# The low-rank decay product written as one 96-row fp32r product, and a different bank for the pooling mix

## The chip, the cores and the metric

The kernel runs on one core of one Trainium2 chip. The core has five engines with a queue each: TensorE (PE in the profile; PEld is its weight load), VectorE (DVE), ScalarE (ACT), GpSimd (POOL) and SyncE (SP), which issues all DMA transfers of this kernel. The metric is the device time of one execution in microseconds (us); the time before is 1222.71 us, the median of three runs (1220.06, 1222.71, 1222.97). PE writes into PSUM, which this kernel divides into banks of 128 partitions x 512 fp32 values; ACT and DVE read a bank and so free it.

## The reference, cut to what matters

One block of a streaming encoder for 1024 tokens and 16 meta tokens, model width 1024. The input is normalised and projected by one wide matrix into `a` (512 columns), `q`, `k` (256), `v`, `r` (512), `lr` (16) and two gates (1024). What the change touches is the decay of the gated linear attention, which comes from the 16 columns `lr`, and the mixing of the pooled `a`, 128 columns to a group:

```
z = einsum('bld,dn->bln', u, w_in)
a, q, k, v, r, lr, ga, gb = split(z, ...)
p = multiscale_pool(a).reshape(B, L, 4, 128)
p = einsum('blgc,gce->blge', p, w_pool_mix).reshape(B, L, 512) * pool_scale
log_a = log_sigmoid((lr @ w_gate_up + b_gate).astype(float32)) / GLA_TAU
...
h = h + hybrid_mixer(rmsnorm(h, norm_mix), ...)
h = h + squared_relu_mlp(rmsnorm(h, norm_ffn), w_ff1, w_ff2)
return rmsnorm(h, norm_final)[:, N_META:]
```

`w_gate_up` has 16 rows and 256 columns, so `lr @ w_gate_up` sums over 16 terms only.

## The kernel before, in words

Most products are made from split operands: a value x is written as hi + lo, where hi is x rounded to fp32r and lo is the rest, and a product is hi·hi + hi·lo + lo·hi, three fp32r matmuls that accumulate in one bank (`mm3`, L280 to L282). The exception here is `log_decay` (L514): it multiplies the unsplit fp32 tiles `wgu` (16 x 256) and `gB[:16]` (the transposed `lr`, 16 x 1024), and `lrT_meta` for the meta tokens, as plain fp32.

The first part of the program is a list of steps, `one`, that `drive` runs through. `start` normalises and transposes the input into `th`/`tl`, makes `v` and `lr` together (`v_tile`, whose last 16 columns go to `lrtok`), and ends with `lr_turn`: three transposes of `lrtok` into `ms` banks, which ACT copies to `lrT_meta` and `gB[:16]` (L415, L420). `pool_open` releases the buffers of `start` and makes those of the pooling stage. Then follow blocks of projections and the work between them: `a_block(0)`, `decays(0)`, `a_block(1)`, `decays(1)`, `mix_block(0)`, `a_block(2)`, `mix_block(1)`, `a_block(3)`, `mix_block(2)`, `k_block(0)`, `mix_block(3)`, the differences, `k_block(1)`, and then the pairs of the remaining projections.

- `a_block` and `k_block` call `project`: three pieces of 264, 264 and 512 columns, 24 products each, every piece in one of the three `mm` banks in turn. ACT evicts each piece (L563 or L597).
- `decays(p)` calls `log_decay` for two halves of 512 columns and for the 16 meta columns, each in one of the three `ms` banks. ACT adds the bias (L515) and makes the logarithm of a sigmoid from absolute value, exponential and logarithm (L516 to L518), DVE joins them (L519), ACT takes the exponential (L528) and SP writes the decays to memory (L529). SP reads them back much later into the tile `g` (L925).
- `mix_block(g)` makes trailing sums of `a` on DVE (L576, L579), splits them into `ph` (ACT L582, DVE L583) and multiplies them by `mw`, one half in an `ms` bank and one in half of the wide pair `sc` (L280 to L282 again, output `b_ms` and `b_sc`). ACT scales both by `pool_scale` (L588).

The order of PE is that of the program as written (PE alone is scheduled by hand). The order of the other engines' queues is made by the framework's scheduler when the kernel is built; each engine then works through its queue strictly in order. Tiles lie on two stacks, left and right; a new tile on a place that was released waits until all users of the old one are done. The weights of the next blocks are split two blocks ahead by ACT (L84) and DVE (L85).

Of the kernel before, what the change touches and what calls it, by code (L numbers as in the profile page):

```python
# [7 lines left out]
F32 = mybir.dt.float32  # L8
F32R = mybir.dt.float32r
U8 = mybir.dt.uint8  # L10
ACT = mybir.ActivationFunctionType
ALU = mybir.AluOpType
AX = mybir.AxisListType

P = 128
D = 1024
SEQ = 1024
META = 16
KT = D // P
HALF = 512  # L20
# [102 lines left out]
def kernel(  # L123
# [3 lines left out]
    nc = tc.nc  # L127
# [3 lines left out]
    w_gate_up, b_gate, gla_norm, w_gla_out, w_out = w_gate_up[0], b_gate[0], gla_norm[0], w_gla_out[0], w_out[0]  # L131
    norm_ffn, w_ff1, w_ff2 = norm_ffn[0], w_ff1[0], w_ff2[0]

    act, dve, pool, pe = nc.scalar, nc.vector, nc.gpsimd, nc.tensor
    left, right = Stack(tc, "left"), Stack(tc, "right")
# [18 lines left out]
    def bank(tag):  # L154
        if tag == "sc":
            sc_n[0] += 1
            return two("sc")[:, sc_n[0] % 2]
        return psp[tag].tile([P, 512], F32, name=f"b_{tag}", tag=tag)
# [25 lines left out]
    gB = left.push("gB", [P, D], F32)  # L184
# [10 lines left out]
    stat = [tiny(16) for _ in range(4)]  # L195
    eps_t = tiny(1)
    pool.memset(eps_t, EPS)
    wgu = left.push("wgu", [16, 256], F32)
    metab = left.push("metab", [P, 5, 16], F32)
    lrT_meta = left.push("lrT_meta", [16, META], F32)  # L200
    raw = Raw(nc, [left.push(f"raw{i}", [P, D], F32) for i in range(2)])
    W1 = Ring(tc, raw, left.push("w1h", [P, 2, D], F32R), left.push("w1l", [P, 2, D], F32R), 2)
    left_ff = left.mark()
# [8 lines left out]
    def f32(ap):  # L212
        return ap.bitcast(F32)

    def col(v, n):
        return v.rearrange("(h p) -> p h", p=P)
# [87 lines left out]
    S, rings = {}, [W1]  # L304
# [56 lines left out]
    def nxt(key):  # L361
        i = S["n" + key]
        S["n" + key] += 1
        return S[key][:, i % S["d" + key]]

    def halves():
        return [slice(h * HALF, (h + 1) * HALF) for h in range(2)]
# [42 lines left out]
            nc.sync.dma_start(v_dram[i, t], o)  # L410

    def lr_turn():
        b = bank("ms")
        pe.transpose(b[:16, :16], S["lrtok"][:16, 8], ident[:16, :16])
        act.activation(lrT_meta, b[:16, :16], ACT.Copy)  # L415
        for h in range(2):
            b = bank("ms")
            for t in range(4):
                pe.transpose(b[:16, t * P : (t + 1) * P], S["lrtok"][:, 4 * h + t], ident)
            act.activation(gB[:16, h * HALF : (h + 1) * HALF], b[:16], ACT.Copy)  # L420


    SPREAD = {
# [7 lines left out]
    def start():  # L431
        act.preload_act_table_set("natural_log_exp_and_others")
        xs = left.push("xs", [P, 4, D], F32)
        us = left.push("us", [P, 3, D], F32)
        S["lrtok"] = left.push("lrtok", [P, 10, 16], F32)
        S["lrraw"] = left.push("lrraw", [P, KT, 16], F32)
        xm = left.push("xm", [META, D], F32)
        um = left.push("um", [META, D], F32)
        mf = left.push("mf", [P, 6, CH], F32)
        S["xr"] = right.push("xr", [P, KT, SEQ], F32)  # L440
        S["vw"] = [right.push(f"vw{i}", [P, 2, KT, n], F32R) for i, n in enumerate((VP, 256))]
        buffer("vo", 3, 2 * P, right)
        load = lambda t: nc.sync.dma_start(xs[:, t % 4], x[t * P : (t + 1) * P, :])
        blank = S["xr"].rearrange("p k c -> p (k c)")[:, -640:]
        pool.memset(blank, 0.0)

        def warm(n, cols=HALF):
            for _ in range(n):
                pe.matmul(bank("ms")[:, :cols], blank[:, HALF:], blank[:, :cols], start=True, stop=True)

        load(0)
        nc.sync.dma_start(um[:1], norm_mix[None, :])
        nc.sync.dma_start(ident, ident_in)
        ask_vw(0)
        nc.sync.dma_start(S["lrraw"], w_in[:, C_LR : C_LR + 16].rearrange("(k p) c -> p k c", p=P))
        pool.memset(xm[:1, :P], 1.0)
        warm(2)
        for c in halves():
            b = bank("mm")
            pe.matmul(b, xm[:1, :P], um[:1, c], start=True, stop=True)  # L460
            dve.tensor_copy(gB[:, c], b)
        warm(2)
        for t in range(8):
            if 0 < t < 6:
                load(t + 2)
            if t == 1:
                nc.sync.dma_start(xm, meta)
            if t == 3:
                W1.top_up()
            u = us[:, t % 3]  # L470
            layer_norm(xs[:, t % 4], u)
            transposed(u, t // 4, OFF[t // 4] + (t % 4) * P, ("ms", "sc"))
            if t == 0:
                load(1)
                load(2)
                warm(10, P)
                load_vw(0)
                ask_vw(1)
            if t == 6:
                layer_norm(xm, um)  # L480
            if t == 1:
                warm(6, P)
            if t == 2:
                load_vw(1)
            if t < 3:
                v_tile(0, t)
            else:
                for i, n in SPREAD[t]:
                    v_tile(i, n)
        transposed(um, 0, 0)  # L490
        v_tile(0, 7)
        v_tile(1, 6)
        v_tile(1, 7)
        v_tile(0, 8)
        v_tile(1, 8)
        lr_turn()
        nc.sync.dma_start(mf, masks)
        pool.tensor_copy(mask, mf)
        nc.sync.dma_start(pscale, col(pool_scale, 4))
        nc.sync.dma_start(bgate, col(b_gate, 2))  # L500
        nc.sync.dma_start(gnorm, col(gla_norm, 4))
        nc.sync.dma_start(wgu, w_gate_up)

    one = []
    step(one, start)
# [5 lines left out]
    def log_decay(lrT, p, n, y, t):  # L511

        b = bank("ms")[:, :n]
        pe.matmul(b, wgu[:, p * P : (p + 1) * P], lrT, start=True, stop=True)  # L514
        act.activation(y, b, ACT.Identity, bias=bgate[:, p : p + 1])  # L515
        act.activation(t, y, ACT.Abs)  # L516
        act.activation(t, t, ACT.Exp, scale=-1.0)
        act.activation(t, t, ACT.Ln, bias=1.0)  # L518
        dve.scalar_tensor_tensor(y, y, 0.0, t, ALU.min, ALU.subtract)  # L519

    META_LOG = (0, 3)

    def decays(p):
        def fn():
            for half, c in enumerate(halves()):
                y = nxt("c")
                log_decay(gB[:16, c], p, HALF, y, nxt("t1"))
                act.activation(y, y, ACT.Exp, scale=1.0 / TAU)  # L528
                nc.sync.dma_start(decay_dram[p, half], y)  # L529
                yield 0.6  # L530
            if p:
                act.activation(gnorm, gnorm, ACT.Copy, scale=0.5)
            log_decay(lrT_meta, p, META, metab[:, META_LOG[p]], metab[:, 4])
            if p:
                tc.keep_in_program_order(act.preload_act_table_set("exp_and_others"))

        return fn

    def pool_open():
        left.pop_to(base)  # L540
        right.pop_to(1)
        buffer("c", 4)
        buffer("t1", 3)
        S["left_t"] = left.mark()
        buffer("a", 2, 1056)
        buffer("s", 2, 1056)
        S["ph"] = left.push("ph", [P, 2, SEQ], F32R)
        mw = S["mw"] = left.push("mw", [P, 2, 4, P], F32R)
        r = raw.load(w_pool_mix.rearrange("g c e -> c g e"), 4 * P).rearrange("p (g e) -> p g e", g=4)
        act.activation(mw[:, 0], r, ACT.Copy)  # L550
        dve.tensor_tensor(mw[:, 1], r, f32(mw[:, 0]), ALU.subtract)
# [17 lines left out]
    def mix_block(g):  # L569
        def fn():  # L570
            a, w, e = pooled[g], WINDOWS[g], SEQ + META
            cur, k = a, 1
            while k < w:
                c = META - (w - 2 * k)
                dst = nxt("s")
                dve.tensor_tensor(dst[:, c:e], cur[:, c:e], cur[:, c - k : e - k], ALU.add)  # L576
                cur, k = dst, 2 * k
            pp = nxt("s")
            dve.scalar_tensor_tensor(pp[:, :SEQ], cur[:, META:e], 1.0 / w, a[:, META:e], ALU.mult, ALU.subtract)  # L579
            wb = (S["mw"][:, 0, g], S["mw"][:, 1, g])  # L580
            for c in halves():
                act.activation(S["ph"][:, 0, c], pp[:, c], ACT.Copy)  # L582
                dve.tensor_tensor(S["ph"][:, 1, c], pp[:, c], f32(S["ph"][:, 0, c]), ALU.subtract)  # L583
            for h, (tag, c) in enumerate(zip(("ms", "sc"), halves())):
                b = bank(tag)
                mm3(b, 1, lambda i: wb, lambda i: (S["ph"][:, 0, c], S["ph"][:, 1, c]))
                o = nxt("c")
                act.activation(o, b, ACT.Copy, scale=pscale[:, g : g + 1])  # L588
                nc.sync.dma_start(pm_dram[g, h], o)
                yield  # L590

        return fn
# [1044 lines left out]
```

## Time and profile before

| | value |
|---|---|
| time, median of 3 runs | 1222.71 us |
| time of the profiled execution | 1222.77 us |
| span of its instructions | 1221.0 us |
| mean granted TensorE clock | 0.999 |
| ACT busy | 572.0 us (47%) |
| DVE busy | 838.9 us (69%) |
| POOL busy | 75.5 us (6%) |
| PE busy on L514, the decay products with `gB` | 4.0 us, 8 instructions |

The span runs from the first to the last instruction of the profiled execution; the 1.77 us around it belong to the time too. In rows of a time line the columns are the start, the duration, the engine, the line, the operation, output and inputs with shapes, the count, and in square brackets how long the engine sat idle before it and what released it. In the chain of waits a row has the start, the length that the piece adds to the chain, and the piece. Durations of matmuls overlap, since they are pipelined: what a matmul costs in a row of others is the distance of starts, which is what the chain shows.

### The profile page before, as it was taken

The numbers are of one execution on the slowest core, as the hardware profiler recorded it, in microseconds if no ns is written. First come the engines' busy times: TensorE is split into PE (matmuls) and PEld (weight loads), VectorE is DVE, ScalarE is ACT, GpSimd is POOL, SyncE is SP. The second block draws the span as 40 slices with busy tenths as digits, with TensorE's granted clock in tenths as the row PEclk, the third lists the DMA queues.
The fourth block names the chain that finished last, engine by engine and source line by source line (L and its number), as shares of the span: only waits on it lengthen the run. The fifth ranks groups of instructions, "written<-read, shape, count | busy, mean of one in ns | idle before, by whom it ended". The sixth has DMA issues, their size and how long they took to land.

```text
span 1221.0 us, 18366 instructions
## 1 busy us (share of the span) xinstructions
PE 1207.9 (99%) x6807; PEld 997.2 (82%) x6807; DVE 838.9 (69%) x1381; ACT 572.0 (47%) x1009; POOL 75.5 (6%) x96
## 2 busy tenths in 40 slices
PE   9999999999999999999999999999999999999997
PEld 6998977778778888788778888888888888888886
DVE  6535657665777569825887677676775887887686
ACT  7627444444456224314655455454554444444544
POOL 0000043222330000000000000000000000000000
PEclk9999999999999999999999999999999999999999
DMA  8313334435247977921244444444569973333532
GB/s 236 93 40 95 118 100 130 147 105 164 81 137 266 318 243 233 323 67 69 104 139 156 141 163 151 150 155 145 172 228 326 332 246 104 96 95 96 171 95 88
DMA packets 153356, 192.76 MB, mean 158 GB/s; under 512 B 12178, under 2 KB 88226, under 8 KB 153267
## 3 DMA queue, kind: packets, MB, share of 16 engines
q1 hardware_dynamic: 153266, 191.59, 48.9%
q8 instruction: 53, 0.87, 0.3%
q14 instruction: 37, 0.30, 0.1%
HBM read 128.62 MB, written 62.93 MB: 157 GB/s over the span
## 4 chain that ended last, share of the span: by engine, by line
PE 89%; DVE 4%; DMA 2%; ACT 2%; issue 2%; POOL 0%; SPq 0%; POOLq 0%; ACTq 0%; DVEq 0%
PE b_mm L280 7%; PE b_mm L282 7%; PE b_mm L281 7%; PE b_y L280 6%; PE b_y L282 6%; PE b_y L281 6%; PE b_oa L282 5%; PE b_oa L281 5%; PE b_oa L280 5%; PE b_z L280 4%; PE b_z L282 4%; PE b_z L281 4%; PE b_sc L280 4%; PE b_ob L281 4%; PE b_ob L282 4%; PE b_ob L280 4%
## 5 line engine op out<-in xcount | busy, mean ns | idle before, releaser
L685 ACT ACTIVATE w1h<-raw 128x512 fp32r<-128x512 f32 x106 | 65.9, 622 | 59.3 <-PE b_y L281 25.3
L686 DVE TENSOR_TENSOR w1l<-raw,w1h 128x512 fp32r<-128x512 f32 x106 | 72.4, 684 | 22.0 <-ACT w1h L685 22.0
L280 PE MATMUL b_sc<-th,w1h 128*128 128x512 f32 x216 | 85.6, 396 | 0.6 <-ACT u2p L1420 0.6
L280 PE MATMUL b_z<-th,w1h 128*128 128x512 f32 x216 | 85.3, 395 | 0.5 <-DVE c L804 0.3
L281 PE MATMUL b_sc<-tl,w1h 128*128 128x512 f32 x216 | 84.9, 393 | 0.0
L281 PE MATMUL b_z<-tl,w1h 128*128 128x512 f32 x216 | 84.3, 390 | 0.4 <-DVE tl L1306 0.4
L282 PE MATMUL b_sc<-th,w1l 128*128 128x512 f32 x216 | 84.4, 391 | 0.0
L685 ACT ACTIVATE w1h<-fs 128x512 fp32r<-128x512 f32 x81 | 51.1, 631 | 70.7 <-PE b_y L281 32.9
L282 PE MATMUL b_z<-th,w1l 128*128 128x512 f32 x216 | 84.1, 389 | 0.0
L686 DVE TENSOR_TENSOR w1l<-fs,w1h 128x512 fp32r<-128x512 f32 x81 | 57.1, 705 | 26.1 <-ACT w1h L685 25.9
L280 PE MATMUL b_mm<-th,w1h 128*128 128x512 f32 (+1 forms) x208 | 72.1, 347 | 0.0
L281 PE MATMUL b_mm<-tl,w1h 128*128 128x512 f32 (+1 forms) x208 | 71.0, 341 | 0.0
L282 PE MATMUL b_mm<-th,w1l 128*128 128x512 f32 (+1 forms) x208 | 71.0, 341 | 0.0
L685 ACT ACTIVATE w1h<-bt 128x512 fp32r<-128x512 f32 x46 | 29.1, 632 | 70.9 <-issue 43.9
L1496 DVE TENSOR_TENSOR bt<-w,w 128x512 f32<-128x512 f32 x80 | 54.6, 683 | 1.0 <-DMA w<-in_w_ff_dram 0.9
L280 PE MATMUL b_mm<-wo,th 128*128 128x512 f32 x128 | 50.4, 393 | 0.0
L282 PE MATMUL b_mm<-wo,tl 128*128 128x512 f32 x128 | 49.9, 390 | 0.0
L281 PE MATMUL b_mm<-wo,th 128*128 128x512 f32 x128 | 49.8, 389 | 0.0
L280 PE MATMUL b_y<-wo,w1h 128*128 128x512 f32 x128 | 49.8, 389 | 0.0
L281 PE MATMUL b_y<-wo,w1h 128*128 128x512 f32 x128 | 49.8, 389 | 0.0
L282 PE MATMUL b_y<-wo,w1l 128*128 128x512 f32 x128 | 49.8, 389 | 0.0
L686 DVE TENSOR_TENSOR w1l<-bt,w1h 128x512 fp32r<-128x512 f32 x46 | 31.7, 690 | 25.6 <-ACT w1h L685 25.6
(405 smaller groups left out, 3334.6 us busy)
## 6 DMA issues: line engine op xcount, KB each, us to landing
hf_dram<-h SPq DMA_DIRECT2D x112, 256.0 KB, 2.1
raw<-hf_dram SPq DMA_DIRECT2D x112, 256.0 KB, 2.6
w<-in_w_ff_dram SPq DMA_DIRECT2D x64, 256.0 KB, 4.5
raw<-in_w_in_dram SPq DMA_DIRECT2D x22, 512.0 KB, 4.3
raw<-in_w_ff_dram SPq DMA_DIRECT2D x16, 512.0 KB, 4.2
rawx<-in_w_ff_dram SPq DMA_DIRECT2D x16, 512.0 KB, 4.2
rawp<-in_w_in_dram SPq DMA_DIRECT2D x10, 512.0 KB, 4.4
xs<-in_x_dram SPq DMA_DIRECT2D x8, 512.0 KB, 4.8
```

What stands on the lines that cost most here:

```text
L280: pe.matmul(ps, ah, bh, start=first and i == 0, stop=False, skip_group_check=more)
L281: pe.matmul(ps, ah, bl, start=False, stop=False, skip_group_check=more)
L282: pe.matmul(ps, al, bh, start=False, stop=last and i == n - 1, skip_group_check=more)
L685: act.activation(hi, a, ACT.Copy)
L686: dve.tensor_tensor(lo, a, f32(hi), ALU.subtract)
L1496: dve.tensor_tensor(bt, w, S["w2"][q[3:]][:, i], ALU.add if q[2] == "+" else ALU.subtract)
```

## The change

The decay product is now made from split operands as well, but in one matmul and not three. A tile `lr` with 96 rows holds the rounded `lr` in rows 0 to 15 and again in rows 64 to 79, and its rest in rows 32 to 47; all other rows are zero. A tile `gu` with 96 rows holds `w_gate_up` rounded in rows 0 to 15 and 32 to 47, and its rest in rows 64 to 79. The sum over the 96 rows is hi·hi + lo·hi + hi·lo. Both tiles are fp32r. They lie on the right stack, where the weights of `v` lay, so the call of `lr_turn` moves from the end of `start` into `pool_open`, behind the release. `wgu` is loaded three times by DMA into a tile of 96 rows that POOL has zeroed, and `lr` is zeroed by POOL as well. `wgu` takes as much room per partition as before and `metab` grows by the room that `lrT_meta` had, so that the tiles behind them keep their places. Apart from this, the first half of each mixing product goes to an `mm` bank instead of an `ms` bank.

```diff
-    wgu = left.push("wgu", [16, 256], F32)
-    metab = left.push("metab", [P, 5, 16], F32)
-    lrT_meta = left.push("lrT_meta", [16, META], F32)
+    wgu = left.push("wgu", [96, 256], F32)
+    metab = left.push("metab", [P, 6, 16], F32)
...
     def lr_turn():
+        def stacked(to, b):
+            act.activation(to[:16], b, ACT.Copy)
+            act.activation(to[64:80], b, ACT.Copy)
+            dve.tensor_tensor(to[32:48], b, f32(to[:16]), ALU.subtract)
+
         b = bank("ms")
         pe.transpose(b[:16, :16], S["lrtok"][:16, 8], ident[:16, :16])
-        act.activation(lrT_meta, b[:16, :16], ACT.Copy)
-        for h in range(2):
+        stacked(S["lr"][:, SEQ : SEQ + META], b[:16, :16])
+        for h, c in enumerate(halves()):
             b = bank("ms")
             for t in range(4):
                 pe.transpose(b[:16, t * P : (t + 1) * P], S["lrtok"][:, 4 * h + t], ident)
-            act.activation(gB[:16, h * HALF : (h + 1) * HALF], b[:16], ACT.Copy)
+            stacked(S["lr"][:, c], b[:16])
...
         pool.memset(blank, 0.0)
+        pool.memset(wgu, 0.0)
...
-        lr_turn()
...
-        nc.sync.dma_start(wgu, w_gate_up)
+        for r in (0, 32, 64):
+            nc.sync.dma_start(wgu[r : r + 16], w_gate_up)
...
-        pe.matmul(b, wgu[:, p * P : (p + 1) * P], lrT, start=True, stop=True)
+        pe.matmul(b, S["gu"][:, p * P : (p + 1) * P], lrT, start=True, stop=True)
...
-                log_decay(gB[:16, c], p, HALF, y, nxt("t1"))
+                log_decay(S["lr"][:, c], p, HALF, y, nxt("t1"))
...
-            log_decay(lrT_meta, p, META, metab[:, META_LOG[p]], metab[:, 4])
+            log_decay(S["lr"][:, SEQ : SEQ + META], p, META, metab[:, META_LOG[p]], metab[:, 4])
...
     def pool_open():
+        right.pop_to(1)
+        S["lr"] = right.push("lr", [96, SEQ + 2 * META], F32R)
+        S["gu"] = right.push("gu", [96, 256], F32R)
+        pool.memset(f32(S["lr"]), 0.0)
+        lr_turn()
+        act.activation(S["gu"], wgu, ACT.Copy)
+        dve.tensor_tensor(S["gu"][64:96], wgu[64:], f32(S["gu"][64:96]), ALU.subtract)
         left.pop_to(base)
-        right.pop_to(1)
...
-            for h, (tag, c) in enumerate(zip(("ms", "sc"), halves())):
+            for h, (tag, c) in enumerate(zip(("mm", "sc"), halves())):
```

PE has as many instructions as before in the same order; only operands and banks differ. This is PE's queue where the second decay block meets the first mixing block, before and of the change (`b_mm`, `b_ms` and `b_sc` are banks, line numbers of the changed file are one lower in `mm3`):

```order
L282 MATMUL b_mm<-th_144,w1l 128x512
L514 MATMUL b_ms<-gB,wgu 128x512 x2
L514 MATMUL b_ms<-lrT_meta,wgu 128x16
L280 MATMUL b_ms<-ph,mw 128x512
L281 MATMUL b_ms<-ph,mw 128x512
L282 MATMUL b_ms<-ph,mw 128x512
L280 MATMUL b_sc<-ph,mw 128x512
```

```order
L281 MATMUL b_mm<-th_140,w1l 128x512
L519 MATMUL b_ms<-lr,gu 128x512 x2
L519 MATMUL b_ms<-lr,gu 128x16
L279 MATMUL b_mm<-ph,mw 128x512
L280 MATMUL b_mm<-ph,mw 128x512
L281 MATMUL b_mm<-ph,mw 128x512
L279 MATMUL b_sc<-ph,mw 128x512
```

No row has moved; the decay products read `lr` and `gu`, and the mixing product of the first half writes an `mm` bank.

On ACT the place is the end of `start` and the beginning of the first projection block: `mw` are the mixing weights, `t2h` is a split operand of a later stage, `a` the evictions of the first two pieces. Before, and of the change:

```order
L550 ACTIVATE mw<-raw_120 128x512
L406 ACTIVATE gB<-b_mm 16x256 x2
L415 ACTIVATE lrT_meta<-b_ms 16x16
L615 ACTIVATE t2h<-xr 128x2048
L420 ACTIVATE gB<-b_ms 16x512 x2
L563 ACTIVATE a<-b_mm 128x264 x2
```

```order
L561 ACTIVATE mw<-raw_116 128x512
L550 ACTIVATE gu<-wgu 96x256
L405 ACTIVATE gB<-b_mm 16x256 x2
L413 ACTIVATE lr<-b_ms 16x16
L414 ACTIVATE lr<-b_ms 16x16
L626 ACTIVATE t2h<-xr 128x2048
L413 ACTIVATE lr<-b_ms 16x512
L414 ACTIVATE lr<-b_ms 16x512
L413 ACTIVATE lr<-b_ms 16x512
L414 ACTIVATE lr<-b_ms 16x512
L574 ACTIVATE a<-b_mm 128x264 x2
```

The copy to `gu` came in ahead of the two evictions to `gB`, and each copy of transposed `lr` is there twice, ahead of the evictions of `a`. DVE's queue has four new subtractions at the same place, two of them behind the split of `t2l`.

SP's queue around the read of the decays into `g`, with the waits of each issue (DMAHW are counters of earlier transfers), before and of the change:

```order
L529 DMA decay_dram<-c 128x512 [waits DMAHW3_49,Activation_49]
L529 DMA decay_dram<-c 128x512 [waits DMAHW4_49,Activation_49]
L925 DMA g<-decay_dram 128x512 [waits DMAHW5_49,DMAHW3_49,PE_49]
L118 DMA raw_120<-in_w_in_dram 128x8x128 [waits DMAHW6_49,DMAHW1_49,DVE_49]
L589 DMA pm_dram<-c 128x512 [waits DMAHW7_49,Activation_49]
```

```order
L534 DMA decay_dram<-c 128x512 [waits DMAHW5_49,Activation_49]
L534 DMA decay_dram<-c 128x512 [waits DMAHW6_49,Activation_49]
L936 DMA g<-decay_dram 128x512 [waits DMAHW5_49,DMAHW7_49,PE_49,Pool_49]
L118 DMA raw_116<-in_w_in_dram 128x8x128 [waits DMAHW3_49,DMAHW0_49,DVE_49]
L600 DMA pm_dram<-c 128x512 [waits DMAHW1_49,Activation_49]
```

The order is the same; the read into `g` now waits for POOL too, whose zeroing of `lr` is its only work at that place: `g` lies where `lr` and `gu` were.

## The prediction

> **What bounds the kernel now.** I read the page first: busy time by engine, then the chain of work that ended last.
>
> ```profile
> PE 1207.9 (99%) x6807; PEld 997.2 (82%) x6807; DVE 838.9 (69%) x1381; ACT 572.0 (47%) x1009; POOL 75.5 (6%) x96
> PE 89%; DVE 4%; DMA 2%; ACT 2%; issue 2%; POOL 0%; SPq 0%; POOLq 0%; ACTq 0%; DVEq 0%
> ```
>
> PE is busy in 99% of the span and carries 89% of the chain. An average hides stages, so the next view is the busy time by stretch, around the two decay blocks and the first mixing (columns: length, then busy us with counts for PE, PEld, DVE, ACT, POOL, granted clock, DMA share, GB/s).
>
> ```profile
> 79.00:92.00 13.00, 13.00 (x84) 11.36 (x84) 2.29 (x1) 4.83 (x8) 0.00 (x0) 1.00 0.13 37
> 92.00:106.00 14.00, 14.00 (x81) 11.50 (x80) 7.79 (x18) 9.80 (x23) 0.00 (x0) 1.00 0.31 94
> 106.00:120.00 14.00, 14.00 (x84) 12.21 (x83) 8.75 (x17) 10.60 (x23) 0.00 (x0) 1.00 0.35 114
> ```
>
> PE's busy time equals the length of each, at a granted clock of 1.00, while ACT and DVE are busy for 10.60 us of 14.00 at most. The waits of PE over the whole span confirm it; the longest after the start-up is this:
>
> ```profile
> PE b_mm L280 <- DVE o L1095: 1.2, 1, 1.2
> PE b_z L280 <- DVE c L804: 0.3, 1, 0.3
> ```
>
> So time that PE no longer needs between 91 and 108 us comes off the end, if everything that feeds PE is early enough to follow. The places themselves, in the chain of waits:
>
> ```profile
> 63.71 0.60 PE b_ms L273 x8
> 64.31 0.32 PE b_mm L280
> ...
> 91.45 2.04 PE b_ms L514 x6
> 93.48 0.32 PE b_mm L280
> ...
> 105.02 2.04 PE b_ms L514 x6
> 107.06 0.46 PE b_ms L280
> 107.52 0.23 PE b_ms L281
> ```
>
> A decay block adds 2.04 us for three products (six records, two for each), and the product behind it is longer than usual: 0.32, and 0.46 where its successor of the same shape has 0.23. The weight loads of the fp32 products show what one pass takes:
>
> ```profile
> 92.34 0.18 PEld L514 LDWEIGHTS b_ms<-gB,wgu 16*128 16x128 f32 x1 [0.24 <-issue]
> 92.77 0.18 PEld L514 LDWEIGHTS b_ms<-lrT_meta,wgu 16*128 16x128 f32 x1 [0.24 <-PE b_ms L514]
> ```
>
> They start 0.43 us apart, so a 512-column fp32 product costs two times 0.43 = 0.86 us, against 0.23 for an fp32r product of that width.
>
> **The decay products.** Before, the two blocks with the product behind each take 2.04 + 0.32 + 2.04 + 0.46 = 4.86 us. After, a block has two 512-column fp32r products and one of 16 columns. No row shows an fp32r product over 96 rows. The nearest is the one over 128 rows, 0.23; the far bound is that it keeps one pass of today's product, 0.43. I take 0.23, since type and width are the same there. For 16 columns the bounds are 0.075 (eight 16-column products in 0.60, the row at 63.71) and the 0.23 of a wide one; I take 0.10, near the first, because its load is as wide. The 0.32 behind the eight short products at 64.31 is as long as that behind the decays, so I leave this extra of 0.20 (0.32 against some 0.12 for a 264-column product, half of the 0.23 of 512) to the short product: it stays. So after: 2 x 0.23 + 0.10 + 0.32 = 0.88 and 2 x 0.23 + 0.10 + 0.43 = 0.99, together 1.87. The gain is 4.86 - 1.87 = **2.99 us**, about 1.48 at the first block and 1.51 at the second. If the extra goes too and the short one takes 0.075, after is 0.655 + 0.765 = 1.42 and the gain 3.44. With passes of 0.43 and a short product of 0.23 after is 1.41 + 1.52 = 2.93 and the gain 1.93.
>
> The Trainium skill, "TensorE: Matmul & The Clock Gate", section "Back-to-back issue gap", gives 131 ns for sustained 512-column products. The trace disagrees, since 512-column products stand 0.23 apart in it; by the page's figure four products would save another 0.4 us, an estimate, and the sum above doesn't use it.
>
> **The start-up of the new tiles.** Zeroing and loading `wgu` come early:
>
> ```profile
> 0.77 0.63 POOL L445 MEMSET xr<- 128x640 f32 x1
> 5.16 3.78 PE L460 MATMUL b_mm<-um,xm 1*128 1x512 f32 x4
> 33.92 0.50 SPq L502 DMA_DIRECT2D wgu<-in_w_gate_up_dram  x1
> ```
>
> At 0.63 us for 640 columns the 256 of `wgu` take 0.25 us on POOL, ahead of the zeroing of `xm` that PE needs at 5.16: hidden. Two more issues on SP cost 2 x 0.50 us at 34 us; behind them stand a `v` store, the mixing weights, which ACT takes at 75.60 (below), and block weights that it takes at 91.26. Hidden by some 40 us.
>
> The place to check is the queue behind the transposes, since ACT and DVE run strictly in order:
>
> ```profile
> 75.60 0.63 ACT L550 ACTIVATE mw<-raw 128x512 fp32r<-128x512 f32 x1 [1.86 <-DMA v_dram<-vo]
> 79.13 0.37 ACT L406 ACTIVATE gB<-b_mm 16x256 f32<-16x256 f32 x1 [2.24 <-PE b_mm L282]
> 79.53 0.17 ACT L415 ACTIVATE lrT_meta<-b_ms 16x16 f32<-16x16 f32 x1
> 79.61 1.90 ACT L615 ACTIVATE t2h<-xr 128x2048 fp32r<-128x2048 f32 x1
> 81.42 1.04 ACT L420 ACTIVATE gB<-b_ms 16x512 f32<-16x512 f32 x2
> 83.13 0.39 ACT L563 ACTIVATE a<-b_mm 128x264 f32<-128x264 f32 x1 [0.67 <-PE b_mm L282]
> 91.26 1.06 ACT L84 ACTIVATE w1h<-raw 128x1024 fp32r<-128x1024 f32 x1 [4.82 <-PE b_mm L281]
> ...
> 81.55 2.29 DVE L616 TENSOR_TENSOR t2l<-xr,t2h 128x2048 fp32r<-128x2048 f32 x1 [4.13 <-ACT t2h L615]
> ```
>
> `lr` lies where the weights of `v` lay, so POOL may zero it only when the last `v` product is done, just before 79.13 at the latest. 1056 columns take 0.63 x 1056/640 = 1.04 us, to 80.2, so ACT's first copy is late by 0.6. Then come one more small copy (0.17) and two more wide ones (1.04, as L420 now), so `t2h` ends at some 82.3, the copies at 84.4, and the eviction of `a` that stood at 83.13 moves to 84.4. DVE splits `t2l` from 82.3 to 84.6 and then subtracts two halves; no row has 16 x 512 on DVE, so I take two of 128 x 512, 1.29 us (the row of L583 at 115.98, below). `lr` is ready at 85.9. PE wants it at 91.45: 5.5 us of room. The copy to `gu` (0.37, the row of L406 with the same columns) falls into the idle 2.24 ahead of 79.13; what is queued behind is only `a`, whose bank is wanted at 93.48, and the weights at 91.26, whose idle of 4.82 shrinks. I cost this at nothing.
>
> **The banks and the two closest margins.** Behind the second decay block ACT works without a hole:
>
> ```profile
> 104.83 1.06 ACT L84 ACTIVATE w1h<-raw 128x1024 fp32r<-128x1024 f32 x1 [2.38 <-PE b_mm L281]
> 106.27 1.39 ACT L515 ACTIVATE c<-b_ms,small 128x512 f32<-128x512 f32 x2
> 110.83 0.68 ACT L588 ACTIVATE c<-b_ms,small 128x512 f32<-128x512 f32 x1
> 119.82 1.06 ACT L84 ACTIVATE w1h<-raw 128x1024 fp32r<-128x1024 f32 x1 [3.35 <-PE b_mm L281]
> ...
> 115.98 1.29 DVE L583 TENSOR_TENSOR ph<-s,ph 128x512 fp32r<-128x512 f32 x2 [1.29 <-ACT ph L582]
> ...
> 114.36 0.39 PE L280 MATMUL b_mm<-th,w1h 128*128 128x512 f32 x1
> 119.84 0.39 PE L280 MATMUL b_ms<-ph,mw 128*128 128x512 f32 x1
> ```
>
> This stretch begins when PE ends `a_block(1)`, so it moves by 1.48 only, while PE behind it moves by 2.99. On the old `ms` bank the first mixing would come at 107.06 - 2.5 = 104.6 and wait for the first L515 to end, 106.27 + 0.7 - 1.48 = 105.5: 0.9 us lost. On an `mm` bank it doesn't wait, since that was emptied in `a_block(1)`. In return the third bank on in the round, that of the 512-column piece of `a_block(2)`, is the one of the mixing product: ACT frees it at 111.51 - 1.48 = 110.0 and PE wants it at 114.36 - 2.99 = 111.4, **1.4 us of room**. The second mixing needs `ph`, ready at 117.27 - 1.48 = 115.8, at 119.84 - 2.99 = 116.85: **1.05 us of room**. Behind that ACT idles 3.35 us ahead of 119.82, so from there it follows PE again and later banks are no closer. Both cost nothing, but they are thin.
>
> **The read of `g`** now waits for the last decay product, since it lies on `lr` and `gu`:
>
> ```profile
> 100.32 0.32 SPq L925 DMA_DIRECT2D g<-decay_dram  x1
> 107.17 0.38 SPq L118 DMA_DIRECT2D raw<-in_w_in_dram  x1
> ```
>
> That product ends near 104.1; the next issue on SP, due at 107.17 - 1.48 = 105.7, waits for DVE anyway. Nothing is lost.
>
> **Sum.** 1222.77 - 2.99 = **1219.8 us**. The profiled execution lies 0.06 above the median of 1222.71, so the forecast is 0.24% below it. A difference of 0.3% (3.67 us, 1219.04) is about what a measurement of this kernel can tell from no change.
>
> **Rivals.**
> - *More goes than I count.* The extra behind the decays belongs to fp32 and leaves with it: 1222.77 - 3.44 = 1219.3. For it speaks the 0.46 at 107.06, against it the 0.32 at 64.31, which stands behind short products as well.
> - *The 96-row product isn't as cheap as one of 128 rows.* By the far bound 1222.77 - 1.93 = 1220.8; for it speaks only that no row shows it.
> - *The closest margins break.* If ACT's decay stretch doesn't move with `a_block(1)`, `ph` comes at 117.27 and PE loses 0.4: 1220.2.
> - *Slower: `lr` comes late.* PE stands at the first decay product until the chain of zeroing, ACT copies and DVE subtractions is done. The price is the lateness beyond 5.5 us of room. It has eaten the gain at 8.5 us and makes the kernel slower by 0.3% at 5.5 + 2.99 + 3.67 = 12.2 us, at 1226.4. POOL's zeroing would have to last over ten times as long as the row at 0.77 makes it, and nothing in the trace does so.
>
> **Chances.** Forecast 0.55, more gain 0.27, dear product 0.08, broken margins 0.06, late `lr` 0.04. The forecast lies 0.8 us above the bound of 1219.04 and the larger gain 0.3. One of the three runs lay 2.65 us below the median (1220.06); if one in three does, two of three, and so a median, are that low in 7 of 27 cases. That puts a quarter of the forecast's chance, half of the larger gain's and a tenth of the next two on the faster side: 0.14 + 0.14 + 0.01, say 0.30. Slower is the late `lr`, 0.04; within 0.3% is the rest, 0.66. The range goes from 1219.8 - 2.65 = 1217.1 to 1221.4, which is the dear product's 1220.8 with 0.6 for the margins on top.
>
> **What would show it.** In the chain of waits the two rows of 2.04 should become about 0.56, the first mixing product should follow at once on an `mm` bank, and PE should wait at no piece of `a_block(2)` and not at the second mixing. `lr` should be ready near 86 us. The second group of pairs and everything later should start 3 us earlier. I am wrong if a record of the 96-row product stands 0.43 from the next, if PE waits for DVE or POOL at the first decay product, or if PE's wait at `b_z` or at L1095 grows by what was gained.

## The result and the profile after

The changed kernel takes **1220.18 us** (median of 16 runs, 1217.32 to 1222.54) against 1222.94 (16 runs, 1220.02 to 1223.62). The ratio is 0.9979, with a 95% interval of 0.9971 to 0.9988. The forecast was 1219.8. The times of both kernels fall into two groups some 2.5 to 3 us apart, which a median mixes: within each, after is 2.5 to 2.6 us ahead, and both profiled executions (1222.77 us before; 1221.39 us after, with a span of 1219.4) belong to the longer one.

The page of after gives busy time and instruction count by engine, then PE's waits between 160 and 182 us:

```profile
PE 1205.1 (99%) x6801; PEld 996.5 (82%) x6801; DVE 841.1 (69%) x1385; ACT 573.8 (47%) x1013; POOL 76.8 (6%) x98
```

```profile
PE b_sc L279 <- ACT u2p L807: 1.0, 1, 1.0
PE b_z L279 <- DVE c L815: 0.5, 1, 0.5
```

PE is 2.8 us less busy and executes six matmuls and six weight loads less (6807 before). The wait for `u2p` is new, and the one for `c` was 0.3. Next the chain of waits of after at the two decay blocks (start, length, what):

```profile
91.50 0.23 PE b_mm L281
91.74 0.48 PE b_ms L519 x3
92.22 0.23 PE b_mm L279
...
103.67 0.48 PE b_ms L519 x3
104.15 0.34 PE b_mm L279
104.48 0.23 PE b_mm L280
```

Where before had 2.04 + 0.32 and 2.04 + 0.46, after has 0.48 + 0.23 and 0.48 + 0.34, together 1.53. So 4.86 - 1.53 = **3.33 us** went here. The timeline of after answers to the start-up of the tiles and the two margins:

```profile
76.63 0.98 POOL L548 MEMSET lr<- 96x1056 f32 x1 [41.51 <-PE b_mm L281]
...
84.42 0.39 ACT L574 ACTIVATE a<-b_mm 128x264 f32<-128x264 f32 x1
...
84.46 1.28 DVE L415 TENSOR_TENSOR lr<-b_ms,lr 16x512 fp32r<-16x512 f32 x2
...
104.27 0.32 SPq L936 DMA_DIRECT2D g<-decay_dram  x1
...
109.33 0.70 ACT L599 ACTIVATE c<-b_mm,small 128x512 f32<-128x512 f32 x1
...
114.56 1.29 DVE L594 TENSOR_TENSOR ph<-s,ph 128x512 fp32r<-128x512 f32 x2 [1.28 <-ACT ph L593]
```

`lr` is ready at 85.74, the mixing bank free at 110.03, `ph` ready at 115.85.

To see where a gain stays, one takes an operation that both programs have and subtracts its start in after from its start in before. Three of them on ACT, with the SP issue that feeds the third, first of before and then of after:

```profile
54.36 0.39 ACT L409 ACTIVATE vo<-b_mm 128x256 f32<-128x256 f32 x1 [1.18 <-DVE lrtok L404]
...
146.21 0.68 ACT L588 ACTIVATE c<-b_ms,small 128x512 f32<-128x512 f32 x1
...
174.34 0.34 SPq L924 DMA_DIRECT2D gi<-q_dram  x1
...
177.03 0.89 ACT L935 ACTIVATE f<-gi 128x512 f32<-128x512 f32 x1 [4.73 <-DMA gi<-q_dram]
```

```profile
54.65 0.38 ACT L408 ACTIVATE vo<-b_mm 128x256 f32<-128x256 f32 x1 [1.18 <-DVE lrtok L403]
...
143.17 0.68 ACT L599 ACTIVATE c<-b_mm,small 128x512 f32<-128x512 f32 x1
...
171.35 0.34 SPq L935 DMA_DIRECT2D gi<-q_dram  x1
...
175.32 0.88 ACT L946 ACTIVATE f<-gi 128x512 f32<-128x512 f32 x1 [6.06 <-DMA gi<-q_dram]
```

The shift is -0.29 at 54 us, 3.04 at 146 and 1.71 at 177: 3.33 were gained and then **1.33 given back** at one place. The read `gi<-q_dram`, which brings q of the first inside (one of four steps of the attention, each with such a read), takes 2.69 us from issue to use before and 3.97 after, and ACT, strictly in order, stands in front of it. From there to the end the shift stays between 1.4 and 2.0, and is 1.63 on the last rows. The sections below call the median of such differences over all operations of ACT and DVE in the 20 us from a time on the *shift* at that time; the shift at 140 less that at 60 us is the *local gain*, the shift at 180 less that at 140 what the read changes.

### The profile page after: what moved, and what is told of

Same layout as the page of the kernel before. It is cut to its first block, busy times and chain, and to the rows that moved or that the text cites. A ratio compares the mean times of both kernels' runs of the same rounds, so it can differ in the third digit from the quotient of the medians.

```text
span 1219.4 us, 18372 instructions
## 1 busy us (share of the span) xinstructions
PE 1205.1 (99%) x6801; PEld 996.5 (82%) x6801; DVE 841.1 (69%) x1385; ACT 573.8 (47%) x1013; POOL 76.8 (6%) x98
## 4 chain that ended last, share of the span: by engine, by line
PE 90%; DVE 4%; DMA 2%; issue 2%; ACT 1%; POOL 0%; SPq 0%; DVEq 0%; ACTq 0%; POOLq 0%
PE b_mm L279 7%; PE b_mm L281 7%; PE b_mm L280 7%; PE b_y L279 6%; PE b_y L280 6%; PE b_y L281 6%; PE b_oa L281 5%; PE b_oa L279 5%; PE b_oa L280 5%; PE b_z L279 4%; PE b_z L280 4%; PE b_z L281 4%; PE b_sc L279 4%; PE b_ob L281 4%; PE b_ob L279 4%; PE b_ob L280 4%
## 5 line engine op out<-in xcount | busy, mean ns | idle before, releaser
L279 PEld LDWEIGHTS b_sc<-th,w1h 128*128 128x128 f32 x216 | 40.5, 188 | 11.8 <-ACT u2p L807 1.4
```

The lines of the kernel that those rows point to most:

```text
L279: pe.matmul(ps, ah, bh, start=first and i == 0, stop=False, skip_group_check=more)
```

## The experiments

The local gain is larger than forecast; I put that down to the extra time behind the short product, which would belong to the fp32 product and leave with it. The loss at 175 us had no theory at first, only two kinds of cause: something in the change, or something that differs from run to run. The first four runs were to tell these apart, and to split the change into its two edits.

### The two kernels again, and the two edits apart

`after_again` and `before_again` are unedited. `stack_ms` is after with the mixing's first half back on `ms`; `fp32_mm` is before with it on `mm`:

```diff
-            for h, (tag, c) in enumerate(zip(("mm", "sc"), halves())):
+            for h, (tag, c) in enumerate(zip(("ms", "sc"), halves())):
```

> The changed kernel unchanged, profiled once more. Both theories agree on the two decay blocks: 0.48 us each in the chain of waits, against 2.04 before, and 3.3 us gained by 119 us. They differ at 171 to 177 us, where the profile of the change gave 1.3 us of it back because the read of q into gi took 3.97 us from issue to use instead of 2.66. Theory A (the transfer's time changes from execution to execution, whatever the kernel): the read takes another time here, anywhere from 2.6 to 4 us, and PE's wait behind u2p follows it. Theory B (the change moves the read into a collision): again close to 3.97 us, and PE waits about 1.0 us for u2p again.

> The kernel before unchanged, profiled once more. Theory A: the read of q into gi may take anything from 2.6 to 4 us here too, so PE may wait over 1 us for u2p in the kernel before as well. Theory B: 2.66 us again and the only wait there is the 0.3 us for c. Both: 2.04 us for each decay block, time ratio to the kernel before 1.000 within 0.1%.

> The change with the first half of each mixing product left on an ms bank. Theory A (most of the gain is the cheap product, the bank move only keeps the second block's share): the first mixing product waits for ACT to have read the first decay bank, 0.9 us by my reading of the prediction, up to 1.3 by the trace of the change (decays done near 104.1, first ACT reading done near 105.5); the gain at 119 us falls from 3.3 to 2.0 to 2.4 us. Rival (the bank move itself does nothing): still 3.3 us at 119 us. Another rival (the mm bank costs something at the 512-column piece): over 3.3.

> The kernel before with the first half of each mixing product on an mm bank, the decay products left in fp32. Theory A: no gain, below 0.1 us at 119 us, since the wait on the ms bank there is at most the 0.23 us by which the first mixing product is longer than its successor. Rival (the bank of the mixing is what held PE): a good part of 3.3 us is gained here. Time ratio 1.000 by theory A, 0.998 by the rival.

Measured (ratio to before, 95% interval, then local gain): after again 0.9975 [0.9964, 0.9985], 3.32 us; before again 0.9998 [0.9987, 1.0009], 0.00; `stack_ms` 0.9991 [0.9979, 1.0002], 1.69, where 2.0 to 2.4 were expected; `fp32_mm` 0.9996 [0.9985, 1.0007], 0.04. So the stacked product alone brings half, since PE then stands at the first mixing. A row of its waits (95 to 130 us) and the chain there:

```profile
PE b_ms L279 <- ACT c L520: 1.5, 1, 1.5
```

```profile
103.62 1.06 ACT w1h L84
104.68 0.48 ACT a L574
105.16 0.59 ACT c L520
105.75 0.04 issue
105.80 0.50 PE b_ms L279
```

ACT has to split a weight and empty a bank of `a` before it reaches the decay's bank. The bank edit is worth nothing by itself and 1.63 us beside the product. The loss at the read came back in both kernels with the stacked product (0.65 and 0.54 us) and in neither of the others. In `after_again` it is half of what it was in after, though the program is the same: the read takes 3.37 us and not 3.97, and PE waits 0.3 us for `u2p` and not 1.0. So its size differs from execution to execution.

### A theory for the loss

The DMA view of the stretch in which the data of that read move (from about 1 us after its issue to its use) has one packet more in after than in before. First before (175.30 to 177.03 us), then after (172.30 to 175.32):

```profile
DMA packets 144, 0.26 MB, mean 152 GB/s; under 512 B 16, under 2 KB 16, under 8 KB 144
...
q1 hardware_dynamic: 144, 0.26, 52.3%
```

```profile
DMA packets 145, 0.28 MB, mean 92 GB/s; under 512 B 16, under 2 KB 16, under 8 KB 144
...
q1 hardware_dynamic: 144, 0.26, 30.9%
q8 instruction: 1, 0.02, 1.8%
```

Both pages count 53 such instruction blocks of 16 KB; 6807 matmuls and as many weight loads make 257 of PE's instructions for each. My theory: the blocks are PE's, and twelve instructions fewer ahead of the read, 1.4 us of PE work at 0.23 us a matmul, put the block that before had just ahead of the read into it. The same packet stands in the reads of `after_again` and `stack_ms`, and in neither of the other two. The rivals: the read suffers because it is issued at another moment, or from something else that the change added.

### What a 96-row product costs

`thrice` issues each decay product three times; `one_term` leaves out the two correction terms and multiplies over the first 16 rows:

```diff
-        pe.matmul(b, S["gu"][:, p * P : (p + 1) * P], lrT, start=True, stop=True)
+        for _ in range(3):
+            pe.matmul(b, S["gu"][:, p * P : (p + 1) * P], lrT, start=True, stop=True)
```

```diff
-        pe.matmul(b, S["gu"][:, p * P : (p + 1) * P], lrT, start=True, stop=True)
+        pe.matmul(b, S["gu"][:16, p * P : (p + 1) * P], lrT[:16], start=True, stop=True)
```

> After, with every decay product issued three times (the result is the same). If a 96-row product of 512 columns costs 0.23 us as the chain of after says, eight more cost 1.84 us and four short ones 0.1 to 0.4: rows at 120 to 160 us come 1.9 to 2.2 us later than in after. By the prediction's rival of a dear product (about 0.5 us) they come 4 us later. The theory of the fetch adds that with 12 matmuls more than after (6 more than before) no block lands in the read of gi, so that nothing is lost between 165 and 180 us and the time is only 0.6 to 1.7 us above that of after; without it 1.9 to 2.2 us above.

> After, with the decay products over the first 16 rows alone: the two correction terms are left out. If the rows of a product cost nothing, which the change lives on, time and chain are those of after: 0.23 us for a 512-column product, rows at 120 to 160 us within 0.1 us, the time within 0.3 us. If 96 rows cost more than 16, rows there come earlier by four times the difference.

The chain of `thrice`, then that of `one_term`:

```profile
91.60 1.61 PE b_ms L520 x9
93.21 0.22 PE b_mm L279
...
104.66 1.62 PE b_ms L520 x9
106.28 0.33 PE b_mm L279
```

```profile
91.47 0.67 PE b_ms L519 x3
92.14 0.32 PE b_mm L279
...
103.67 0.67 PE b_ms L519 x3
104.34 0.43 PE b_mm L279
```

Four wide and two short products more add 1.61 - 0.48 = 1.13 us to a block: 0.23 for a wide one leaves 0.11 for a short one that stands behind another. (`pad_short`, below, bears this out: its blocks, with three more short products each, take 0.82 us, 0.11 more for each.) Rows at 140 us come 2.24 us later than in after by local gain (1.09 against 3.33), as expected; the dear product (4 us) falls. The time is 0.9992 of before [0.9983, 1.0002].

`one_term` **missed** what I expected: it has fewer rows and its blocks are slower, by 0.19 us inside each and 0.09 behind it, a local gain of 2.77 instead of 3.33. (Its time, 0.9983 of before [0.9972, 0.9995], can't be told from that of after.) The products behind have the 0.32 and 0.43 that I had forecast for after, and so has `fp32_mm` (before has 0.32 and 0.46). So 0.09 of the extra behind the decays in before come neither from fp32, as I had put it above, nor from the short product, as in the prediction: they come with 16-row products between 128-row ones, and so do the 0.19 inside; 96 rows don't pay them. The eight short products on which the prediction leaned have 16 rows as well, as their row in the time line of before says:

```profile
63.64 0.67 PE L273 MATMUL b_ms<-ident,um 16*128 16x16 f32 x8
```

The other 0.11 of the extra stay in after, and are as much as a short product costs in `thrice` and `pad_short`. The Trainium skill, "TensorEngine Tiling (Array Packing)", section "Key Properties", says that a change of tiling mode, not of the tile alone, drains TensorE; these rows fit that, if 96 rows count as the full array and 16 do not, though no record here names the mode.

### Moving the block of instructions without the change

Four kernels alter PE's count alone. `pad_short` issues the 16-column decay products four times, `after_warm13` has 13 filler products in place of 10 at the start (a filler is a product whose result is overwritten; it is two records); both bring after back to the count of before. `before_warm7` takes three fillers out of before, so that it has the count of after and nothing else of the change. `thrice`, above, has 12 matmuls more than after.

```diff
-            pe.matmul(b, S["gu"][:, p * P : (p + 1) * P], lrT, start=True, stop=True)
+        for _ in range(4 if n == META else 1):
+            pe.matmul(b, S["gu"][:, p * P : (p + 1) * P], lrT, start=True, stop=True)
```

```diff
-                warm(10, P)
+                warm(13, P)
```

> After, with each 16-column decay product issued four times instead of once, so that TensorE executes as many instructions (matmuls and weight loads: 6 of each more) ahead of the first inside as in before. Theory of the fetch (TensorE's instructions come in 16 KB blocks over the same DMA engines as data; the change took 6 matmuls out, so that one block now lands in the middle of the read gi<-q_dram, which it delays): the block moves back ahead of the read, the read takes 2.5 to 2.7 us from issue to use instead of 3.4 to 4.0, ScalarE's and VectorE's rows beyond 180 us keep all of the gain that they have at 140 us, and the time is 0.3 to 1.0 us below that of after, less 0.1 to 0.6 us for six short products. Rival (the read is slow because it is issued at another moment, or for a reason in the change's other instructions): a block still in the read, 3.3 to 4.0 us, 0.5 to 1.3 us lost between 165 and 180 us, time 0.1 to 0.6 us above that of after.

> After, with 13 filler products at the start in place of 10, which brings TensorE's count of instructions ahead of the first inside back to that of before without touching the decays. Theory of the fetch: the block comes 0.4 to 0.9 us ahead of the read's issue, the read takes 2.5 to 2.7 us, the local gain of 3.3 us at 120 to 160 us (against this run's own rows at 60 us) is kept beyond 180 us within 0.1 us; the start is 0 to 0.4 us longer, and the time 0.2 to 1.0 us below that of after. Rival: 0.6 to 1.3 us lost again between 160 and 180 us, time that of after or up to 0.4 us above it.

> The converse of the fetch theory, without any of the change: before, with 7 in place of 10 filler products at the start of the program (they write a bank that is overwritten; nothing of the result is left out), which takes 6 matmuls and 6 weight loads out of TensorE's stream, as many as the change does. Theory of the fetch: relative to the read gi<-q_dram the 16 KB block comes 1.4 us later than in before, falls 0.5 to 0.9 us behind its issue, the read takes 3.0 to 3.5 us instead of 2.5 to 2.7, and 0.3 to 0.7 us are lost between 160 and 180 us, though the decay blocks are those of before. Rival (the loss belongs to the stacked product or to its other instructions): block or not, the read takes 2.5 to 2.7 us and nothing is lost there. The start of the program may be 0 to 0.4 us shorter in either case; the time is within 0.8 us of before's.

`before_warm7` by its timeline, its DMA view of the stretch in which the read moves, and its waits of PE between 160 and 185 us:

```profile
174.40 0.34 SPq L924 DMA_DIRECT2D gi<-q_dram  x1
...
177.91 0.88 ACT L935 ACTIVATE f<-gi 128x512 f32<-128x512 f32 x1 [5.56 <-DMA gi<-q_dram]
```

```profile
q1 hardware_dynamic: 144, 0.26, 36.5%
q8 instruction: 1, 0.02, 2.1%
```

```profile
PE b_sc L280 <- ACT u2p L796: 0.5, 1, 0.5
PE b_z L280 <- DVE c L804: 0.4, 1, 0.4
```

The kernel before, without the change but with its instruction count, has the slow read (3.51 us), the new wait for `u2p` and a loss of 0.82 us. I had expected 3.0 to 3.5 us and 0.3 to 0.7 us; the shift ends at -0.97. It is the one variant that is slower than before, 1.0014 [1.0004, 1.0023]; that ratio also depends on how many executions of each have the late start of the last section, so the loss is read from the trace. And `after_warm13`, in the same two views:

```profile
171.51 0.34 SPq L935 DMA_DIRECT2D gi<-q_dram  x1
...
174.05 0.88 ACT L946 ACTIVATE f<-gi 128x512 f32<-128x512 f32 x1 [4.71 <-DMA gi<-q_dram]
```

```profile
DMA packets 144, 0.26 MB, mean 159 GB/s; under 512 B 16, under 2 KB 16, under 8 KB 144
...
q1 hardware_dynamic: 144, 0.26, 59.2%
```

2.54 us, no block, and the local gain of 3.32 is kept whole. `pad_short` has a local gain of 2.73, since six more short products cost 0.60, reads in 2.71 and loses 0.07; what it saves at the read the products take again, and its time, 0.9981 of before [0.9971, 0.9990], is not below that of after. That of `after_warm13` is 0.9978 [0.9967, 0.9988], its profiled execution 1219.63 us against 1221.39 and 1220.55 of after. All eleven profiled executions that read `gi` in this way, from the packet records of their traces (us; the first three columns count from the read's issue):

```
kernel         block starts   last data packet   use in ACT   change of shift, 140 to 180
thrice            -0.96             2.22            2.54           +0.22
before_again      -0.81             2.15            2.47           +0.20
after_warm13      -0.78             2.19            2.54           +0.02
fp32_mm           -0.68             2.35            2.67            0.00
pad_short         -0.63             2.38            2.71           -0.07
before            -0.42             2.34            2.69          (reference)
one_term          +0.52             2.56            3.04           -0.40
stack_ms          +0.68             2.73            3.24           -0.54
after_again       +0.73             2.91            3.37           -0.65
before_warm7      +0.94             2.99            3.51           -0.82
after             +1.41             3.45            3.97           -1.33
```

A block takes 0.88 to 1.37 us. One that starts ahead of the issue does no harm; one behind it lengthens the read by 0.1 to 0.3 us less than it is late (last packet against some 2.3), and the loss follows. That the blocks are PE's can be counted: in all eleven traces this one starts when PE has begun 2187 to 2197 of its matmuls and weight loads, though the clock then stands anywhere from 170.7 to 175.3 us. With that the rivals fall: the moment of the read is 174.3 to 174.4 us in both `before` and `before_warm7`, and none of the change's other instructions is in `before_warm7`.

### The read taken out, and a version to beat both

`direct_q` is after with q of the first inside (one of 4, not 16 as the text below has it) sent from its tile straight into `gi`; `before_direct` does the same to before, and `direct_warm7` is `direct_q` with 7 fillers.

```diff
-        nc.sync.dma_start(q_dram[d, half], o)
+        nc.sync.dma_start(S["gi"][:, 2] if (d, half) == (0, 0) else q_dram[d, half], o)
...
-        nc.sync.dma_start(gi[:, 2], q_dram[p, half])
+        if (p, half) != (0, 0):
+            nc.sync.dma_start(gi[:, 2], q_dram[p, half])
```

> After, with q of the first inside (one of the 16) sent by one DMA straight into gi in place of a write to q_dram and a read back. If what is lost between 165 and 180 us is the wait for that read, the waits of TensorE for u2p and c there (1.0 and 0.5 us in after) go, rows beyond 180 us keep the 3.0 to 3.3 us of local gain, and the time is 0.5 to 1.3 us below that of after. If something else on ScalarE or VectorE is late there, the loss of 0.6 to 1.3 us stays and the time is that of after within 0.3 us.

> Before, with q of the first inside sent straight into gi, as in direct_q. If the way by q_dram costs something in itself, and not by the collision alone, rows beyond 180 us come 0.3 to 0.6 us earlier against the rows at 140 us (direct_q gained 0.61 us there) and the time is that much below before's. If what direct_q won there was the collision alone, rows there stay within 0.1 us and the time is before's.

> direct_q with 7 filler products in place of 10: an attempt at the best version. Where the fillers end later than the data that TensorE needs next (in the profile of after by about 0.6 us), the start is up to 0.38 us shorter (3 x 0.126 us); where they end with them, nothing changes; and with the read of gi gone, a later block of instructions has nothing to hit there. Time 0 to 0.4 us below that of direct_q. If the shorter filling lets TensorE fall back to half speed, the start is 1 us or more longer.

`direct_q`: 0.9978 [0.9968, 0.9987], local gain 3.32, no wait of PE from 160 to 182 us, and not only no loss but 0.61 us more from 140 to 200 us. `before_direct` gains the same 0.61 there, so the way by DRAM costs that much even undisturbed; but it gives 0.50 back near 490 us, at a place that I didn't follow, and ends at 1.0 [0.9989, 1.001]. `direct_warm7`: 0.9975 [0.9964, 0.9985]; its start isn't shorter than after's (shift at 60 us -0.44 against -0.29), so fewer fillers brought nothing there. No version is measurably ahead of after by its ratio, though 0.5 to 1.3 us had been expected of `direct_q` and 0.2 to 1.0 of `after_warm13`. In the traces, counted from each one's rows at 60 us, the last rows have gained 3.71 us in `after_warm13` and 4.25 in `direct_q`, against 1.92 in after and 2.87 in `after_again`.

## Why the prediction was right, and where it was not

- **The bound.** Right. PE is 99% busy, and what it no longer needed at 91 to 104 us reached the operations behind it in full: 3.04 on the clock at 146 us, 3.33 against the rows at 54.
- **The decay products.** The mechanism was right and the sum short by 0.34: 0.88 + 0.99 = 1.87 forecast, 0.71 + 0.82 = 1.53 measured. 0.23 for a wide product over 96 rows was right (`thrice`), the bound of 0.43 far off. Mis-sized was, twice each, the short product with the extra behind it: 0.10 + 0.20 forecast, 0.02 + 0.11 measured (0.48 - 2 x 0.23 in the block's row; 0.23 - 0.12 and 0.34 - 0.23 on the product behind). The step "I leave this extra of 0.20 to the short product: it stays" failed for 0.09 of it. `one_term` shows that these belong to 16-row products, and the row at 64.31, from which the step was read, stands behind 16-row products too. The rival of a larger gain was the right one for this place (bound 3.44), though for another reason than the one it gave.
- **The start-up of the tiles.** Right: 85.74 against 85.9, PE doesn't wait at the first decay product. The place of `lr` was free sooner than I took it: POOL, idle until PE released it, began at 76.63.
- **The bank and the margins.** Right in kind: the bank free at 110.03 (forecast 110.0), `ph` at 115.85 (115.8), no wait of PE. The wait that the `mm` bank avoids was 1.5 us rather than 0.9. Here the prediction's own working is off: it has the first mixing come at 107.06 - 2.5 = 104.6, but 1.48 at each block ahead of it give 107.06 - 2.96 = 104.1, as in its paragraph on the read of `g`, and a wait of 1.4.
- **The read of `g`.** Right: it was issued at 104.27 (104.1 forecast) and delayed nothing.
- **"Everything later should start 3 us earlier."** This step failed. I had named `b_z` as a place where the gain could go, but saw no reason; where it went was the read of `gi`. The section on the change counts PE's rows, which are as many as before; the page counts what PE executes, and an fp32 product is two records. Twelve instructions less moved a block of instructions onto a read that had no room, and 1.33 us (0.65 in the second profile) went back.
- **The time.** 1222.77 + 0.29 - 3.33 + 1.33, and 0.08 more that go at some 620 us, give 1221.14 for the profiled execution, which took 1221.39; the last 0.25 lie behind the last rows. The 0.29 at the start isn't the change's: the shift at 60 us is -0.45 to -0.03 in nine other profiles with the same start, `before_direct` among them with -0.39. So it is partly luck that the forecast came out near the median: two errors had opposite signs, 0.34 too little gained and 0.65 to 1.33 lost unseen. The upper end of the range adds 0.6 for the margins, which the rival prices at 0.4; nothing rests on it.

## What to carry to other kernels

Work taken from the bound engine is worth what the path behind it can still follow, and the first thing to be met there may be a DMA with no room; look for the loads that are issued less than their own duration ahead of their use. An edit that changes PE's instruction count moves its later blocks of instructions against the data, so a microsecond either way may have nothing to do with what the edit was for: compare with a variant that has the same count. Here a block of cheap products among 128-row ones was 0.28 us shorter with 96 rows, most of them zeros, than with 16.

## What the runs showed of the hardware

**Blocks of instructions share the road with data.** A 16 KB packet of the queue that the profile calls "instruction" took 0.88 to 1.37 us at this read; one in the middle of a 256 KB read held back eight of its 128 packets of 2 KB: in after all others had landed 2.39 us behind the issue and these by 3.45. The Trainium skill, "Runtime: NRT & Kernel Launch", section "Instruction fetch mechanics", says that instructions come in blocks of 16 KiB (256) by a DMA queue of the sequencer's own, which agrees with 257 a block here, and that the cost of crossing from one to the next is "mostly hidden". It was hidden for PE, whose waits there name only `u2p` and `c`; for the data it cost up to 1.33 us.

**The start has two modes.** The first rows of PE in `before_again`, two of before a little later, and the stretch from 5 to 9 us in the windows, of before and then of `before_again` (length, then busy us with counts for PE, PEld, DVE, ACT, POOL, granted clock, DMA share, GB/s):

```profile
4.87 1.98 PE L460 MATMUL b_mm<-um,xm 1*128 1x512 f32 x4
6.78 1.98 PE L449 MATMUL b_ms<-xr 128*128 128x512 f32 x4
```

```profile
8.87 3.78 PE L449 MATMUL b_ms<-xr 128*128 128x512 f32 x4
...
13.27 0.60 PE L266 MATMUL b_ms<-ident,us 128*128 128x128 f32 x4
```

```profile
5.00:9.00 4.00, 4.00 (x6) 1.29 (x5) 1.40 (x6) 2.18 (x5) 0.00 (x0) 1.00 1.18 283
5.00:9.00 4.00, 3.76 (x8) 1.21 (x8) 2.76 (x7) 2.38 (x6) 0.00 (x0) 1.00 1.16 289
```

In before four of these records take 3.78 us and in `before_again` 1.98, of the same program; the shift is 2.72 by 20 us and stays. PE goes to full speed at about 5 us in the one and between 12 and 13 in the other, at a granted clock of 1.00 in both. Three of the fourteen profiled executions have the early start (`before_again`, `fp32_mm` and `direct_q`, with a shift of 2.44 to 2.98 at 20 us), the others the late one. That this makes the two groups of times in every kernel is inferred from its size. The Trainium skill, "TensorE: Matmul & The Clock Gate", section "What's actually happening", has a clock gate that opens after a busy window of some 3.4 us, of a window that runs freely, so that the moment depends on where in it the first product falls. PE's first record is at 1.46 us, so an opening at 5 fits one such window; the 12 to 13 us of the other mode are later than it gives, and no run here shows why.
